# A list scheduler that prices changes of tile shape and GpSimd beside VectorE, and ranks the r, v and adaLN steps between units 3 and 4

## The chip, the cores and the metric

One core of a Trainium2 chip. The metric is the device time of one execution in microseconds; the kernel's time is the median of its runs.

## The reference

A decoder trunk of two layers on 256 tokens of width 1024, in float32. Each sub-layer's input is modulated by adaLN, and its output goes through a DeepNorm post-norm:

```
h = x * (1 + scale) + shift
x = LayerNorm(alpha * x + (1 + gate) * f(h))
```

Layer 0 has RWKV-7 time mixing and then a dense SwiGLU of width 2816. The time mixing, which the change is about, is

```
r, k, v = h @ w_rkv + shifted(h) @ w_lerp
w, a, g = three low-rank products of h
per head of 64:  state = state*decay + (state@-kk) kk*a + v k ;  y = state @ r
y = (normalize(y) + bonus) * g ;  out = y @ w_out
```

Then come a shared key and value projection, dilated attention in three groups of heads, and a mixture of 8 experts of width 3584, two for each token. The scale, shift and gate rows all come from one product of the condition vector with a large matrix (`ada_w`), row by row; they are called adaLN rows here, with an index.

## The kernel before, in words

Every product is made in float32 from three passes over halves: ScalarE casts a weight tile to `whi`, VectorE (in places GpSimd) subtracts to get `wlo`, and `mm3` multiplies hi by hi, lo by hi and hi by lo. Nearly every compute instruction is issued by one helper (line 190), loads by `load` (line 119), so the profile's lines don't tell the places apart; the tile names do.

The time mixing is cut into 8 units: four groups of four heads (`c_`), each with two token tiles of 128 (`t`). `unit` (line 869) is a generator; four lanes run at a time, so units 0 to 3 are a first wave, and 4 to 7 take lanes as they come free. A unit computes decay and gates (`sg`), the masked products of its chunk (`SM`), a triangular inverse by block steps (`E`, `T`, `X`), the state (`ST`), the output `Y`, its normalization (`ysum`, `yss`, then Newton steps in `yny` and `yna`), adds bonus and bias, multiplies with the gate product (in `psb`), transposes and leaves the halves `ygh` and `ygl`.

Beside the units run other generators. `rv_task` (line 1192) makes r and v from streamed weights (`x0` and `x2` operands). `ada_lane` (line 377) computes the adaLN rows 3, 4, 2 and 12 from `rawa` loads by `ada_pe` (line 321). `wo_task` (line 1229) is the product with w_out, 96 products in all, 12 for each of the eight row blocks `k`, into four banks of PSUM; block `k` needs `ygh` of units of group `k // 2`. It begins only when all v are there, the gate row is broadcast and the adaLN lane has finished (`ada_left`), whose bank it takes over. `splitter` and `loader` bring the weights of k, r, v and w_out in that order, two tiles ahead of the product. `pn_task` is the post-norm (`u`, `bnst`, `ln_*`, then `f_xh` and `f_xl`, the operands of the FFN), and the `f0` tasks make the first column block of the FFN. The rest of the FFN and the experts are in program order. Attention runs in a second list scheduling.

The order is set by `spin` (line 1324). Each generator yields the engine of its next step and the tiles that it needs. `spin` takes the step with the least estimated start; where starts are equal, as when an engine's queue is the limit, the least rank goes first. Ranks: units 0 to 7 by number, `rv_task` 100, `yg_task` 101, `wo_task` 102, `ada_lane` 103, and up to 110 for `f0`. Starts come from a model: `Engine.cost` (line 133) estimates each instruction's duration and a clock for each engine is kept. The model also keeps an estimate of TensorE's clock (`ham`), into which columns count, and `pick` uses the same starts where a step may go to one of several engines. What `spin` decides is fixed at build time as the order on each engine's queue.

```
best = ((at, order), k_)   # at: need[0].start(need[1:]), order: the rank
yield lambda: len(vsb) == 8 and "gate" in pre and not ada_left[0]   # wo_task
```

Of the kernel before, what the change touches and what calls it, by code (L numbers as in the profile page):

```python
# [91 lines left out]
def tile_kernel(ctx: ExitStack, tc: tile.TileContext, cst_d, att_d, x, c, ada_w, ada_b, ln_g, ln_b, mu, w_rkv,  # L92
# [4 lines left out]
    clk = {"PE": 0.0, "V": 0.0, "SC": 0.0, "GP": 0.0, "DMA": 0.0}  # L97
# [22 lines left out]

    TICK = 3413.0
    HAMT, LAT = 3250, 150
    ham = {"tick": 0, "n": 0, "warm": False, "col": -1}
    grp = {"all": 0.0}
    past = []

    class Engine:
# [5 lines left out]
        def cost(self, op, o, w, start):  # L133
            n = 1
            for d_ in o.shape[1:]:
                n *= d_
            if self.nm == "PE":
                passes = (2 if op == "transpose" else 4) if w.dtype == F32 else 1
                tick = start // TICK
                if tick != ham["tick"]:  # L140
                    ham["warm"] = tick == ham["tick"] + 1 and ham["n"] >= HAMT
                    ham["tick"], ham["n"] = tick, 0
                k, m, col = w.shape[0], o.shape[0], o.start_partition()
                cold = 1 if ham["warm"] else 2
                n0 = ham["n"]
                if m <= 64:
                    t0 = max(start, grp["all"], grp.get(col, 0.0))
                    alt = ham["col"] not in (-1, col)
                    ham["col"] = col
                    ham["n"] += passes * n * k / (128 if not alt else 256 if m > 32 else 512)  # L150
                    grp[col] = t0 + passes * max(n, m) / 2.4 * cold
                    past.append((t0, ham["n"] - n0))
                    return t0 - start + passes / 4 * (64 + n / 4) * cold
                ham["col"] = -1
                ham["n"] += passes * n * k / 128
                past.append((start, ham["n"] - n0))
                grp["all"] = max([start] + list(grp.values())) + passes * max(n, m) / 2.4 * 1.02 * cold
                return grp["all"] - start
            if op == "memset":
                return 60 + n * 0.8  # L160
            if self.nm == "V" and op == "reduce_sum":
                n = 256
            if self.nm == "SC":
                return 55 + n * 0.82 + (0 if op == "copy" else 80)
            return {"V": 70 + n / 0.96, "GP": 60 + n * 2.2 + (70 if n < 512 else 0)}[self.nm]

        def start(self, aps, o=None):
            return max([clk[self.nm]] + [rdy.get(r.tensor.name, 0.0) for r in aps] + (
# [1023 lines left out]
    def rv_task():  # L1192

        yield lambda: len(ksb) == 2
        for j, (kind, c_, i, q) in enumerate(parts):
# [6 lines left out]
                ps = mmt(RV.index((c_, i)) % 2, (128, 2, 256))  # L1202
                ps = [ps[:, 0], ps[:, 1]]
            yield lambda: xvn[i] > q * 4 + 3
            yield PE, hi, lo, xl, ps[0], ps[1]
            for k in range(4):
                kk = q * 4 + k
                for t in range(2):
# [115 lines left out]
    def spin(others, n_units=0, idle=None, ahead=()):  # L1324
# [5 lines left out]
        while True:  # L1330
# [7 lines left out]
            for k_, (order, g, need) in tasks.items():  # L1338
# [2 lines left out]
                    moved = True  # L1341
                if need is None or callable(need):
                    continue
                if isinstance(need[0], int):
                    order, need = need[0], need[1:]
                at = need[0].start(need[1:]) - (AHEAD if ahead and order in ahead else 0)
                if best is None or (at, order) < best[0]:
# [46 lines left out]
    with tc.manual_schedule(engines={mybir.EngineType.PE, mybir.EngineType.DVE, mybir.EngineType.Activation,  # L1394
                                     mybir.EngineType.Pool}):
        spin([(-5, mod_task()), (-4, kvar_task()), (-3, k_task()), (-2.2, splitter()), (51, loader()), (-4.5, lora_task()), (ORD[0], lorag_task()),
                 (ORD[1], rvvar_task(0)), (ORD[2], rvvar_task(2)), (100, rv_task()), (101, yg_task()), (102, wo_task()),
                 (103, ada_lane(LANE)), (104, pre_task()), (105, pn_task(0)), (106, pn_task(1)),
                 (107, f0_load_task()), (108, f0_split_task()), (109, f0_task(0)), (110, f0_task(1))], 8)
    bg_add(*[i for i in ADAS if i not in LANE + LATE])  # L1400
    a_stack.close()
# [24 lines left out]
    xh, xl = pre["fx"]  # L1426
# [808 lines left out]
```

## Time and profile before

| | |
|---|---|
| median of 3 runs | 1843.85 us (1843.07 to 1847.41) |
| profiled execution | 1846.92 us |
| its span | 1845.2 us |
| mean granted clock of TensorE | 0.964 |
| TensorE busy (weight loading) | 1715.7 us, 93% (1368.3 us, 74%) |
| VectorE, ScalarE, GpSimd busy | 1497.0, 1120.4 and 296.6 us |
| read from HBM | 496.07 MB |

The times in the rows are counted from the start of the span; the profiled execution is 3.07 us above the median and 1.7 us above its span. An idle time in front of an instruction stands in brackets, with what ended it. A granted clock of 1.00 is 2.4 GHz.

### The profile page before, as it was taken

How to read it: one execution, taken by the hardware profiler on the slowest of the kernel's cores; microseconds unless marked ns; L12 is line 12 of the kernel's file. 1: busy time of each engine (PE TensorE's matmuls, PEld its weight loads, DVE VectorE, ACT ScalarE, POOL GpSimd, SP SyncE). 2: the span in 40 equal slices, each digit the busy share in tenths (PEclk: the TensorE clock that was granted, in tenths of full speed). 3: DMA queues.
4: the chain of work that ended last, by engine and by line, in shares of the span. 5: the costliest groups of instructions: out<-in, count | busy, mean ns of one | idle time of the engine just before them, and what ended most of it. 6: DMA issues, size and time to landing. Idle time of an engine off the chain costs nothing. (4 is left out here: it accounts for less than half of the span.)

```text
span 1845.2 us, 26366 instructions
## 1 busy us (share of the span) xinstructions
PE 1715.7 (93%) x9828; PEld 1368.3 (74%) x9828; DVE 1497.0 (81%) x2044; ACT 1120.4 (61%) x1447; POOL 296.6 (16%) x222
## 2 busy tenths in 40 slices
PE   6998998869998888979999999999999999999896
PEld 3676776558876666778888888888788787788674
DVE  2786786389886768579899898998888988988888
ACT  3443342236553656438777777877777777777674
POOL 0012222044532785250000000000000000000200
PEclk8998998889998999979999999999999999999998
DMA  9551153559894574568999999999999999999880
GB/s 330 155 160 30 54 164 116 150 189 357 296 354 151 194 256 154 195 230 293 334 352 368 357 349 380 348 360 332 345 368 340 352 345 349 352 344 359 311 320 24
DMA packets 213564, 498.94 MB, mean 270 GB/s; under 512 B 14634, under 2 KB 28818, under 8 KB 213428
## 3 DMA queue, kind: packets, MB, share of 16 engines
q1 hardware_dynamic: 212564, 494.03, 75.7%
q0 software_dynamic: 864, 3.15, 0.5%
q8 instruction: 79, 1.29, 0.3%
q14 instruction: 57, 0.47, 0.1%
HBM read 496.07 MB, written 1.06 MB: 269 GB/s over the span
## 5 line engine op out<-in xcount | busy, mean ns | idle before, releaser
L190 DVE TENSOR_TENSOR wlo<-raw,whi 128x1024 fp32r<-128x1024 f32 x800 | 991.6, 1277 | 138.0 <-ACT whi L190 123.7
L190 ACT CAST whi<-raw 128x1024 fp32r<-128x1024 f32 x808 | 823.9, 1048 | 291.9 <-PE mmb L190 221.2
L190 PE MATMUL mmb<-wlo,xeh 128*128 128x512 f32 x896 | 355.9, 397 | 5.9 <-DVE wlo L190 5.2
L190 PE MATMUL mmb<-whi,xeh 128*128 128x512 f32 x896 | 352.5, 394 | 0.0
L190 PE MATMUL mmb<-whi,xel 128*128 128x512 f32 x896 | 351.6, 392 | 0.0
L190 PEld LDWEIGHTS mmb<-wlo,xeh 128*128 128x128 f32 x896 | 168.4, 188 | 48.3 <-DVE wlo L190 14.9
L190 PEld LDWEIGHTS mmb<-whi,xeh 128*128 128x128 f32 x896 | 168.4, 188 | 34.2 <-ACT whi L190 0.2
L190 PEld LDWEIGHTS mmb<-whi,xel 128*128 128x128 f32 x896 | 168.4, 188 | 32.6
L190 PE MATMUL psb<-wlo,ah 128*128 128x512 f32 x448 | 176.7, 394 | 1.5 <-DVE wlo L190 1.5
L190 PE MATMUL psb<-whi,al 128*128 128x512 f32 x448 | 174.7, 390 | 0.0
L190 PE MATMUL psb<-whi,ah 128*128 128x512 f32 x448 | 161.8, 391 | 0.0
L190 POOL TENSOR_TENSOR macc<-macc,gate 128x1024 f32<-128x1024 f32 x2 | 5.7, 2889 | 924.8 <-ACT gate L190 924.8
L190 POOL TENSOR_TENSOR acc<-acc,raw 128x512 f32<-128x512 f32 (+1 forms) x62 | 128.2, 2082 | 74.2 <-DVE acc L190 42.9
L190 PEld LDWEIGHTS psb<-wlo,ah 128*128 128x128 f32 x448 | 84.1, 188 | 24.6 <-DVE wlo L190 6.2
L190 PEld LDWEIGHTS psb<-whi,ah 128*128 128x128 f32 x448 | 83.5, 188 | 18.8 <-ACT whi L190 1.6
L190 PEld LDWEIGHTS psb<-whi,al 128*128 128x128 f32 x448 | 84.2, 188 | 16.4
L190 PE MATMUL mmb<-whi,f_xl 128*128 128x512 f32 (+1 forms) x192 | 72.1, 375 | 1.1 <-DVE f_xl L190 1.1
L190 PE MATMUL mmb<-whi,f_xh 128*128 128x512 f32 (+1 forms) x192 | 72.7, 379 | 0.0
L190 PE MATMUL mmb<-wlo,f_xh 128*128 128x512 f32 (+1 forms) x192 | 72.0, 375 | 0.2 <-DVE wlo L190 0.2
L190 ACT CAST ah<-psb 128x512 fp32r<-128x512 f32 x56 | 32.6, 583 | 60.3 <-PE psb L190 60.2
L190 ACT ACTIVATE e_s<-mmb 128x512 f32<-128x512 f32 x56 | 33.5, 599 | 44.8 <-PE mmb L190 44.8
L190 DVE TENSOR_TENSOR e_s<-e_s,mmb 128x512 f32<-128x512 f32 x56 | 38.2, 683 | 22.5 <-PE mmb L190 22.2
(417 smaller groups left out, 2589.3 us busy)
## 6 DMA issues: line engine op xcount, KB each, us to landing
raw<-in_moe_w_gu_dram SPq DMA_DIRECT2D x192, 1024.0 KB, 6.6
raw<-in_moe_w_down_dram SPq DMA_DIRECT2D x83, 1024.0 KB, 6.1
raw<-in_moe_w_gu_dram SPq DMA_DIRECT2D x60, 512.0 KB, 7.0
raw<-in_moe_w_down_dram SPq DMA_DIRECT2D x56, 512.0 KB, 6.0
raw<-in_ada_w_dram SPq DMA_DIRECT2D x37, 512.0 KB, 5.3
rawa<-in_ada_w_dram SPq DMA_DIRECT2D x35, 512.0 KB, 4.2
raw<-in_ada_w_dram SPq DMA_DIRECT2D x15, 1024.0 KB, 7.8
raw<-in_ffn_w_gu_dram SPq DMA_DIRECT2D x21, 512.0 KB, 5.3
```

Source lines behind the costliest of these rows:

```text
L190: return fn(*a, **kw)
```

## The change

Two things change; what is computed stays the same. First, the scheduler's model. On TensorE 170 ns are added whenever the class of the tile's shape (rows and columns of the weights: up to 32, up to 64, or 128) differs from that of the product before. Products into alternating column groups count in full towards the estimate of the clock, where they counted for a half or a quarter. An operation on VectorE is estimated longer by 0.6 of the time for which GpSimd's estimated work reaches into it. Second, the ranks: the product steps of `rv_task` and all steps of `ada_lane` go from 100 and 103 to 3.5, and `spin` takes a rank that is no integer. Both list schedulings are drawn up anew by this model, attention's too.

```
--- before.py
+++ after.py
@@ -120,6 +120,7 @@
 
     TICK = 3413.0
     HAMT, LAT = 3250, 150
+    CHG, GPF = 170, 0.6
     ham = {"tick": 0, "n": 0, "warm": False, "col": -1}
     grp = {"all": 0.0}
     past = []
@@ -143,26 +144,38 @@
                 k, m, col = w.shape[0], o.shape[0], o.start_partition()
                 cold = 1 if ham["warm"] else 2
                 n0 = ham["n"]
-                if m <= 64:
-                    t0 = max(start, grp["all"], grp.get(col, 0.0))
-                    alt = ham["col"] not in (-1, col)
-                    ham["col"] = col
-                    ham["n"] += passes * n * k / (128 if not alt else 256 if m > 32 else 512)
-                    grp[col] = t0 + passes * max(n, m) / 2.4 * cold
-                    past.append((t0, ham["n"] - n0))
-                    return t0 - start + passes / 4 * (64 + n / 4) * cold
-                ham["col"] = -1
-                ham["n"] += passes * n * k / 128
-                past.append((start, ham["n"] - n0))
-                grp["all"] = max([start] + list(grp.values())) + passes * max(n, m) / 2.4 * 1.02 * cold
-                return grp["all"] - start
+                shp = tuple(32 if v <= 32 else 64 if v <= 64 else 128 for v in (k, m))
+                if shp != ham.get("shape"):
+                    ham["shape"] = shp
+                    start0, start = start, start + CHG
+                    grp["all"] = max([grp["all"]] + list(grp.values())) + CHG
+                    return self.pe(op, o, passes, n, k, m, col, cold, n0, start) + CHG
+                return self.pe(op, o, passes, n, k, m, col, cold, n0, start)
             if op == "memset":
                 return 60 + n * 0.8
             if self.nm == "V" and op == "reduce_sum":
                 n = 256
             if self.nm == "SC":
                 return 55 + n * 0.82 + (0 if op == "copy" else 80)
-            return {"V": 70 + n / 0.96, "GP": 60 + n * 2.2 + (70 if n < 512 else 0)}[self.nm]
+            if self.nm == "V":
+                d_ = 70 + n / 0.96
+                return d_ + GPF * min(d_, max(0.0, clk["GP"] - start))
+            return 60 + n * 2.2 + (70 if n < 512 else 0)
+
+        def pe(self, op, o, passes, n, k, m, col, cold, n0, start):
+            if m <= 64:
+                t0 = max(start, grp["all"], grp.get(col, 0.0))
+                alt = ham["col"] not in (-1, col)
+                ham["col"] = col
+                ham["n"] += passes * n * k / 128
+                grp[col] = t0 + passes * max(n, m) / 2.4 * cold
+                past.append((t0, ham["n"] - n0))
+                return t0 - start + passes / 4 * (64 + n / 4) * cold
+            ham["col"] = -1
+            ham["n"] += passes * n * k / 128
+            past.append((start, ham["n"] - n0))
+            grp["all"] = max([start] + list(grp.values())) + passes * max(n, m) / 2.4 * 1.02 * cold
+            return grp["all"] - start
 
         def start(self, aps, o=None):
             return max([clk[self.nm]] + [rdy.get(r.tensor.name, 0.0) for r in aps] + (
@@ -1202,7 +1215,7 @@
                 ps = mmt(RV.index((c_, i)) % 2, (128, 2, 256))
                 ps = [ps[:, 0], ps[:, 1]]
             yield lambda: xvn[i] > q * 4 + 3
-            yield PE, hi, lo, xl, ps[0], ps[1]
+            yield 3.5, PE, hi, lo, xl, ps[0], ps[1]
             for k in range(4):
                 kk = q * 4 + k
                 for t in range(2):
@@ -1341,7 +1354,7 @@
                     moved = True
                 if need is None or callable(need):
                     continue
-                if isinstance(need[0], int):
+                if isinstance(need[0], (int, float)):
                     order, need = need[0], need[1:]
                 at = need[0].start(need[1:]) - (AHEAD if ahead and order in ahead else 0)
                 if best is None or (at, order) < best[0]:
@@ -1395,7 +1408,7 @@
                                      mybir.EngineType.Pool}):
         spin([(-5, mod_task()), (-4, kvar_task()), (-3, k_task()), (-2.2, splitter()), (51, loader()), (-4.5, lora_task()), (ORD[0], lorag_task()),
                  (ORD[1], rvvar_task(0)), (ORD[2], rvvar_task(2)), (100, rv_task()), (101, yg_task()), (102, wo_task()),
-                 (103, ada_lane(LANE)), (104, pre_task()), (105, pn_task(0)), (106, pn_task(1)),
+                 (3.5, ada_lane(LANE)), (104, pre_task()), (105, pn_task(0)), (106, pn_task(1)),
                  (107, f0_load_task()), (108, f0_split_task()), (109, f0_task(0)), (110, f0_task(1))], 8)
     bg_add(*[i for i in ADAS if i not in LANE + LATE])
     a_stack.close()
```

The compiled orders show what it moves. TensorE around unit 4's first products, which are those into `psb` from `w2t` with `lw` and `a2t` with `la` (the first number behind `SV`, `SM`, `U`, `T`, `E` or `Y` is the unit's, a last one of three or four digits tells buffers apart; `x2h` and `x2l` are operands of the v projection). Before:

```order
L190 MATMUL psb_1902<-ART_3_1399,BKT_3_1839 128x128 x4
L190 MATMUL psb_1927<-SV_2_1913,SM_2_1421 64x64 x4
L190 MATMUL psb_1938<-w2t_265,lw_267 128x256
L190 MATMUL psb_1938<-a2t_266,la_268 128x256
L190 MATMUL psb_1951<-U_2_1918,E_2_1529 64x64 x4
L190 MATMUL psb_1961<-T_3_1949,SM_3_1854 64x64 x8
L190 MATMUL psb_1972<-g2t_868,lga_269 128x256
L190 MATMUL psb_1972<-w2t_265,lw_267 128x256
L190 MATMUL psb_1977<-SV_2_1913,BKn_2_1233 128x128 x2
L190 MATMUL psb_1981<-cst_79,Y_1_1715 128x128 x2
```

and with the change:

```order
L203 MATMUL mmb_2222<-whi_2187,x2h_256 128x256
L203 MATMUL mmb_2222<-wlo_2188,x2h_256 128x256
L203 MATMUL mmb_2222<-whi_2187,x2l_257 128x256
L203 MATMUL psb_2348<-w2t_265,lw_267 128x256
L203 MATMUL psb_2348<-a2t_266,la_268 128x256
L203 MATMUL psb_2356<-w2t_265,lw_267 128x256
L203 MATMUL psb_2356<-a2t_266,la_268 128x256
L203 MATMUL mmb_617<-cst_79,row_2365 128x128 x2
L203 MATMUL psb_2373<-U_3_2255,E_3_1646 64x64 x4
```

Before, unit 4 begins among the steps of units 2 and 3, and 144 of the 384 products of r and v come behind it. With the change all of them are ahead: unit 4 begins behind the last v product, with unit 5 beside it, and next to it stands one of unit 3's late steps.

TensorE around unit 7's end: the last adaLN products (`rawa`), the first ones of w_out (`ygh`, `ygl`) and the transposes of unit 7's output (`cst` with `Y_7`). Before:

```order
L190 MATMUL mmb_3698<-rawa_3837,cs_act_96 32x256 x4
L190 MATMUL mmb_3698<-rawa_3860,cs_act_96 32x256 x4
L190 MATMUL mmb_3698<-cst_79,row_3892 128x128 x2
L190 MATMUL mmb_3901<-whi_2666,ygh_1125 128x512
L190 MATMUL mmb_3901<-wlo_2667,ygh_1125 128x512
L190 MATMUL mmb_3901<-whi_2666,ygl_1126 128x512
L190 MATMUL psb_3910<-g2t_868,lga_269 128x256
L190 MATMUL psb_3910<-w2t_265,lw_267 128x256
L190 MATMUL mmb_3902<-whi_2666,ygh_1125 128x512
L190 MATMUL mmb_3902<-wlo_2667,ygh_1125 128x512
L190 MATMUL mmb_3902<-whi_2666,ygl_1126 128x512
L190 MATMUL psb_3917<-cst_79,Y_7_3763 128x128 x2
```

and with the change:

```order
L203 MATMUL mmb_3531<-whi_3986,ygh_1264 128x512
L203 MATMUL mmb_3531<-wlo_3987,ygh_1264 128x512
L203 MATMUL mmb_3531<-whi_3986,ygl_1265 128x512
L203 MATMUL mmb_3532<-whi_3966,ygh_1264 128x512
L203 MATMUL mmb_3532<-wlo_3967,ygh_1264 128x512
L203 MATMUL mmb_3532<-whi_3966,ygl_1265 128x512
L203 MATMUL mmb_3532<-whi_3986,ygh_1264 128x512
L203 MATMUL mmb_3532<-wlo_3987,ygh_1264 128x512
L203 MATMUL mmb_3532<-whi_3986,ygl_1265 128x512
L203 MATMUL psb_4037<-g2t_835,lga_269 128x256
L203 MATMUL psb_4037<-w2t_265,lw_267 128x256
L203 MATMUL psb_4046<-cst_79,Y_7_3817 128x128 x2
```

Before, the adaLN products are followed by w_out's first two sets of three and then by unit 7's transposes, and 90 of the 96 products of w_out come behind. With the change no adaLN product is left here, and these w_out products are the last of the first token tile; 12 products, all of the second tile, come behind the transposes.

VectorE around unit 7's end: `wlo` are the splits of w_out's tiles (the last two of the FFN's), `u0` is the post-norm. Before:

```order
L190 TENSOR_TENSOR Y_7_3763<-Y_7_3763,psb_3910 128x256
L190 TENSOR_TENSOR ygl_1126<-psb_3917,ygh_1125 128x2x128
L190 TENSOR_TENSOR wlo_3929<-raw_2709,whi_3928 128x1024
L190 TENSOR_TENSOR wlo_3947<-raw_2784,whi_3946 128x1024
L190 TENSOR_TENSOR wlo_3971<-raw_3938,whi_3970 128x1024
L190 TENSOR_TENSOR wlo_3986<-raw_3956,whi_3985 128x1024
L190 TENSOR_TENSOR wlo_4007<-raw_3977,whi_4006 128x1024
L190 TENSOR_TENSOR wlo_4020<-raw_3995,whi_4019 128x1024
L190 TENSOR_TENSOR u0_4043<-mmb_3901,gate1_3699 128x512
L190 SCALAR_TENSOR_TENSOR u0_4043<-xres_3260,u0_4043 128x512
L190 TENSOR_TENSOR wlo_4038<-raw_4023,whi_4037 128x1024
```

and with the change, from unit 6's last steps on, and then the end of unit 7:

```order
L203 TENSOR_TENSOR wlo_3902<-raw_3857,whi_3901 128x1024
L203 TENSOR_TENSOR ygl_1265<-psb_3922,ygh_1264 128x2x128
L203 TENSOR_REDUCE ysum_7_3961<-Y_7_3817 128x4
L203 TENSOR_SCALAR ysum_7_3961<-ysum_7_3961 128x4
L203 TENSOR_TENSOR Y_7_3817<-Y_7_3817,ysum_7_3961 128x256
L203 TENSOR_TENSOR wlo_3967<-raw_3890,whi_3966 128x1024
...
L203 TENSOR_TENSOR Y_7_3817<-Y_7_3817,vsb1_2675 128x256
L203 TENSOR_TENSOR u0_4035<-mmb_3531,gate1_3455 128x512
L203 TENSOR_TENSOR Y_7_3817<-Y_7_3817,psb_4037 128x256
L203 SCALAR_TENSOR_TENSOR u0_4035<-xres_3405,u0_4035 128x512
L203 TENSOR_TENSOR wlo_4042<-raw_4005,whi_4041 128x1024
L203 TENSOR_TENSOR ygl_1265<-psb_4046,ygh_1264 128x2x128
```

Before, six splits stand between `ygl` of unit 7 and the first step on `u0`. With the change splits stand between the steps of units 6 and 7, and the first step on `u0` stands ahead of the last steps of unit 7. On the load queue (SP) w_out's last four tiles stay behind all adaLN loads and behind that of `bb`, as they were behind the adaLN loads before.

## Rows read from the trace of the kernel before

**Rows 1.** Stretches of the span: columns are stretch and its length, then as named

```profile
core 0: us, PE busy (x) PEld busy (x) DVE busy (x) ACT busy (x) POOL busy (x), PEclk, DMA share, GB/s
59.00:180.00 121.00, 109.67 (x1153) 88.37 (x1152) 89.28 (x244) 47.63 (x113) 18.58 (x32) 0.95 0.39 117
180.00:294.00 114.00, 103.69 (x1287) 81.67 (x1286) 89.48 (x289) 43.59 (x113) 28.50 (x45) 0.94 0.34 107
294.00:345.00 51.00, 43.32 (x471) 29.29 (x472) 18.91 (x67) 12.26 (x33) 7.25 (x13) 0.78 0.46 136
...
394.00:584.00 190.00, 187.74 (x926) 153.78 (x924) 153.76 (x134) 102.26 (x120) 69.09 (x28) 1.00 0.82 299
...
823.00:1832.00 1009.00, 997.85 (x4575) 813.01 (x4574) 898.62 (x858) 754.39 (x821) 12.42 (x4) 1.00 0.92 332
```

**Rows 2.** Timeline of ScalarE, first instruction of units 0 and 4 (start, duration, instruction)

```profile
59.46 0.38 ACT L190 ACTIVATE sg<-psb 128x256 f32<-128x256 f32 x1 [0.52 <-PE psb L190]
...
180.41 0.39 ACT L190 ACTIVATE sg<-psb 128x256 f32<-128x256 f32 x1 [1.18 <-PE psb L190]
```

**Rows 3.** Timeline of VectorE, first inverse step of unit 7

```profile
293.52 0.76 DVE L190 STREAM_TRANSPOSE T<-E 128x256 f32<-128x256 f32 x2
```

**Rows 4.** Timeline of VectorE, 345 to 394 us

```profile
345.18 0.42 DVE L190 TENSOR_TENSOR ygl<-psb,ygh 128x256 fp32r<-128x256 f32 x1 [1.99 <-ACT ygh L190]
348.12 1.23 DVE L190 TENSOR_TENSOR wlo<-raw,whi 128x1024 fp32r<-128x1024 f32 x1 [2.52 <-ACT whi L190]
...
362.66 1.22 DVE L190 TENSOR_TENSOR wlo<-raw,whi 128x1024 fp32r<-128x1024 f32 x1 [1.39 <-ACT whi L190]
364.71 0.69 DVE L190 TENSOR_TENSOR u<-mmb,gate 128x512 f32<-128x512 f32 x1 [0.82 <-PE mmb L190]
...
366.14 1.22 DVE L190 TENSOR_TENSOR wlo<-raw,whi 128x1024 fp32r<-128x1024 f32 x1
...
369.21 1.22 DVE L190 TENSOR_TENSOR wlo<-raw,whi 128x1024 fp32r<-128x1024 f32 x1
...
370.95 0.67 DVE L190 TENSOR_TENSOR u<-mmb,gate 128x512 f32<-128x512 f32 x1
...
393.14 0.84 DVE L190 TENSOR_TENSOR f_xl<-modtmp,f_xh 128x512 fp32r<-128x512 f32 x1 [0.69 <-ACT f_xh L190]
```

**Rows 5.** Timeline of TensorE, 337 to 379 us

```profile
337.19 1.08 PE L190 MATMUL mmb<-rawa,cs_act 128*32 128x256 f32 x8 [2.01 <-DMA rawa<-in_ada_w_dram]
...
339.10 0.78 PE L190 MATMUL mmb<-whi,ygh 128*128 128x512 f32 x1
...
368.21 0.39 PE L190 MATMUL mmb<-wlo,ygh 128*128 128x512 f32 x1
368.45 0.40 PE L190 MATMUL mmb<-whi,ygl 128*128 128x512 f32 x1
378.27 1.11 PE L190 MATMUL psb<-cst,u 128*128 128x128 f32 x4 [9.43 <-DVE u L190]
```

**Rows 6.** Groups of TensorE's instructions, 294 to 372 us (busy us, mean ns, idle before)

```profile
L190 PE MATMUL mmb<-whi,ygh 128*128 128x512 f32 x32 | 14.1, 440 | 0.6 <-ACT whi L190 0.6
L190 PE MATMUL mmb<-wlo,ygh 128*128 128x512 f32 x32 | 13.7, 427 | 1.0 <-DVE wlo L190 1.0
L190 PE MATMUL mmb<-whi,ygl 128*128 128x512 f32 x32 | 13.3, 415 | 0.0
L190 PE MATMUL mmb<-rawa,cs_act 128*32 128x256 f32 x104 | 10.1, 465 | 4.8 <-DMA rawa<-in_ada_w_dram 4.8
```

**Rows 7.** Timeline of VectorE, with GpSimd busy beside it and without

```profile
277.97 0.83 DVE L190 SCALAR_TENSOR_TENSOR sg<-kQ,sg 128x256 f32<-128x256 f32 x1
278.83 0.42 DVE L190 TENSOR_TENSOR kQ<-kQ 128x256 f32<-128x256 f32 x1
```

**Rows 8.** Waits of TensorE's weight loading, 60 to 370 us (total, times, longest)

```profile
PEld psb L190 <- issue: 29.4, 70, 2.0
```

**Rows 9.** Timelines of VectorE and GpSimd near the end of attention

```profile
792.54 8.48 DVE L190 SCALAR_TENSOR_TENSOR ln_a<-ln_y,ln_v 128x1 f32<-128x1 f32 x1
...
791.15 4.69 POOL L190 TENSOR_TENSOR wlo<-raw,whi 128x1024 fp32r<-128x1024 f32 x2
```

## The prediction

> **What bounds the kernel now.** I read the table of stretches first [rows 1]. From 394 to 584 us (the FFN) TensorE is busy 187.74 of 190 us, and from 823 to 1832 us (the experts) 997.85 of 1009, both at a granted clock of 1.00, 2.4 GHz. Both are written in program order and are not rearranged, so whatever moves their first product moves the end by the same amount. The time to win or lose lies in the two list-scheduled parts, up to 394 us and 764 to 823 us.
>
> In the first part I read the milestones of the units. Unit 0 begins at 59.46 us and unit 4, which opens the second wave, at 180.41 (their sigmoids on ScalarE) [rows 2]. Unit 7 starts its triangular inverse at 293.52 [rows 3]. Then I followed VectorE from there [rows 4]: unit 7's result is split into its halves at 345.18. Only after that come six splits of w_out, the first at 348.12, the last at 362.66, and at 364.71 the first `u` of the post-norm. The last operand of the FFN (`f_xl`) ends at 393.14 + 0.84 = 393.98. So from unit 7's result to the first `u` is 364.71 - 345.18 = 19.5 us, in which VectorE does 6 x 1.23 us and otherwise waits, 2.52 us before the first.
>
> Why is w_out so late? TensorE's list [rows 5] has the last adaLN products at 337.19, behind a wait of 2.01 us for their load, and the first product with `ygh` at 339.10. `wo_task` starts only when the adaLN lane is finished. That gate, not the data, set the start: on four lanes, unit 7 can only begin when units before it are done, so w_out's first rows had long been there. TensorE then idles 9.43 us before 378.27, waiting for `u`.
>
> **The change, part by part.**
> *Planner numbers.* They compute nothing and cost nothing on the chip; they only alter the order. Five operations go from ScalarE to VectorE, and attention gets 24 more of the dummy products that keep the clock up, all in TensorE's waits: 0.
>
> *Ranks.* The r, v and adaLN steps now go ahead of units 4 to 7 when TensorE could take either. Counting the compiled orders (a 4-byte product is two records), 1249 records lay between the first products of unit 0 and unit 4, now 1538; between there and unit 7's inverse 1234, now 1041; from there to its final transposes 455, now 437; from there to the first FFN product 118, now 32. The adaLN products are all before unit 7's inverse, so w_out is let go there: of its 96 products 90 came behind unit 7's transposes, now 12.
>
> Term 1, the gap. From `ygl` of unit 7 to `u` 19.5 us goes, and the two later splits (366.14 and 369.21, 1.22 us each, between steps of the layer norm) [rows 4] go too: -19.5 - 2.4 = **-21.9 us**. As a check the other way round: what must follow `ygl` now is 12 products and token tile 1's half of the post-norm. The 12 cost at most 12 x 0.44 = 5.3 us by the longest mean [rows 6], say 4; from tile 1's first `u` at 370.95 to 393.98 is 23.0 us [rows 4]. Together 27 of the 48.8 us that it takes now: -21.4.
>
> Term 2, the splits put elsewhere. Six of the eight splits now stand between steps of units 6 and 7 on VectorE. Each is 1.23 us [rows 4] and, where it waits for its cast or load, holds what is queued behind it: the unit's Newton steps. Bounds 0 (in VectorE's waits: it is busy 18.91 of 51 us from 294 to 345 [rows 1]) and 6 x 1.23 = 7.4; half of them on the path: **+3.7 us**.
>
> Term 3, more work ahead of unit 7. Net 96 records come in front of its inverse, in the main the 104 adaLN products: 10.1 us by their row [rows 6] if nothing hides them. TensorE idles 121 - 109.67 = 11.3 us in the first wave and 114 - 103.69 = 10.3 in the second [rows 1], so some of it fills gaps: bounds 0 and 10.1, I take **+4 us**.
>
> Term 4, w_out's products between unit 7's steps. Each set of three delays a small product by at most its own time, 27 sets in all; against it, the adaLN waits such as 2.01 us are gone and the clock of 0.78 in that stretch [rows 1] should rise with more work. I set these against each other: 0. Here rows can be read in two ways. By TensorE's busy time, 43.32 of 51 us [rows 1], only 7.7 us are free for products that take at least (14.1 + 13.7 + 13.3) / 96 x 81 = 34.7 us of busy time at the mean of [rows 6], or 81 x 0.23 = 18.6 us by their spacing at the full clock (the last two begin at 368.21 and 368.45 [rows 5]). By weight loading, 29.29 of 51, there are 21.7 us free. The first reading would give back 18.6 - 7.7 = 10.9 us, the second none; I take the second, since the unit's small products overlap one another. The Trainium skill (Trainium Kernel Development and Optimization, section Performance Expectations) says that matmul busy time is a bad metric because matmuls are pipelined and that the busy share of weight loading is a good one; by that rule the term stays 0, and no row here alone settles it.
>
> Tile shapes: by the new rule's classes the order of the first part has 227 changes instead of 240. What a change costs no row shows alone; the nearest is TensorE's weight loading waiting for nothing but issue, 29.4 us in 70 waits, 0.42 each [rows 8]. 13 x 0.42 = 5.5 us at most, 0 at least; I take 0, since these waits lie on a unit's own chain too. The Trainium skill (TensorEngine Tiling (Array Packing), section Key Properties) says a change of tiling mode drains the engine, which would put the value nearer to the 5.5.
>
> VectorE beside GpSimd: the same kind of 256-wide operation takes 0.83 us beside GpSimd and 0.42 without [rows 7]. The new price steers splits and adds, but not the units' own GpSimd steps, and the VectorE instructions up to unit 7's inverse are 592 in both orders: 0, at best some 5 us.
>
> Term 5, attention. The adds of the last adaLN rows move, the out-projection of the second token tile stands behind the router of the first, and three normalizations move to GpSimd. The end of attention already has such a stall: a tiny VectorE operation took 8.48 us at 792.54 while GpSimd was splitting weights from 791.15 [rows 9]. Such a stall can go (-8.3) or come again; the order of neither shows which. **0**, bounds -5 and +8.
>
> Sum: -21.9 + 3.7 + 4 + 0 + 0 = **-14.2 us**. The profiled execution took 1846.92 us (span 1845.2 and 1.7 around it), so it would be 1832.7; it stands 3.07 above the median, so against that **1830 us**.
>
> **The rivals.**
> A, slower: the second wave starts late and does not catch up. 289 more records before unit 4, at 109.67 / 1153 = 0.095 us each [rows 1], are 27.5 us, or 30 at that stretch's busy share of 0.91. If the second wave then still takes its 113 us, because the chain of each unit and not TensorE's queue sets it, and has no r, v or adaLN products to fill its waits, unit 7's inverse is at 324 instead of 293.5. Then +30 - 18 = +12: 1856 us. For it: VectorE was busy 89.48 of those 114 us [rows 1], and its unit work is the same; with units 4 and 5 starting together near unit 3's end, fewer units are under way at the seam to fill one another's waits. Against it: TensorE is busy 103.69 of 114, so its queue counts, and 193 records fewer are worth 193 x 0.081 = 15.6 us. It decides once the inverse begins after 294 + 18 = 312 us. Chance 0.14.
>
> B, little gained: w_out is let go but takes TensorE's time from unit 7 (10.9 us given back, above), or its loads come late: its last four stand behind 19 adaLN loads on SP's queue and behind one of `bb`, which waits for a buffer that unit 7 still reads. -14.2 + 10.9 = -3.3, or half of it; between 1834 and 1841. Chance 0.22.
>
> C, more: the steps of the second wave also run better, with 5.5 us of tile changes and some 7 us of VectorE's doubled operations gone: 1830 - 12.5 = 1817. Chance 0.14.
>
> D, the change of order eats its own gain in attention: +8 there, 1838. Chance 0.08. That it does not do what it says is excluded by the order, which moves as its words tell.
>
> **How the numbers follow.** The forecast has 0.42, rivals A to D 0.14, 0.22, 0.14 and 0.08. What counts as no change is 0.3%, 5.5 us: the fence is 1838.3. The forecast falls below it in nearly all cases (0.40), C in all (0.14), B in seven of ten (0.15), D in half (0.04), together 0.73; A is above 1849.4, nearly all of it slower: 0.13; the rest, 0.14, lies between. The range, 1813 to 1848, holds the forecast with its bounds (-27 and -2), B, D and C, and leaves out A and a better C.
>
> **What would show it.** Unit 4's first sigmoid near 205 us; unit 7's inverse near 298; w_out's splits and products inside unit 6 and 7's steps, with hardly a wait between unit 7's `ygl` and `u`; the first full stretch of the FFN 14 us earlier; the experts unchanged in length. An inverse after 312, a split that waits several us for its load ahead of unit 7's Newton steps, or an attention stage 8 us longer would make it wrong.

## The result, and the profile after

The changed kernel takes 1856.3 us (median of 4 runs, 1854.97 to 1859.77), 1.0054 times the kernel before (95% interval 1.0034 to 1.0074). The forecast was 1830 us and the range 1813 to 1848: wrong in sign and outside the range, and at the time that rival A gave, 1856 us. The execution profiled here took 1859.77 us, with a span of 1858.0 us, 12.8 above that of before.

The table of stretches of the changed kernel, with the columns of [rows 1], cut at its own milestones:

```profile
core 0: us, PE busy (x) PEld busy (x) DVE busy (x) ACT busy (x) POOL busy (x), PEclk, DMA share, GB/s
60.00:180.00 120.00, 109.74 (x1140) 90.04 (x1139) 87.61 (x228) 45.37 (x108) 20.75 (x32) 0.93 0.35 105
180.00:215.00 35.00, 34.31 (x403) 29.92 (x402) 20.12 (x58) 14.86 (x33) 4.62 (x8) 1.00 0.49 163
215.00:325.00 110.00, 89.82 (x1009) 62.14 (x1008) 71.25 (x246) 31.73 (x90) 23.45 (x38) 0.84 0.44 135
325.00:361.00 36.00, 34.87 (x402) 26.63 (x403) 19.88 (x52) 13.86 (x32) 6.29 (x10) 1.00 0.19 60
...
404.00:594.00 190.00, 188.02 (x928) 154.37 (x927) 153.02 (x133) 101.27 (x120) 67.99 (x27) 1.00 0.82 299
...
835.00:1845.00 1010.00, 998.35 (x4574) 813.14 (x4574) 897.98 (x856) 753.48 (x819) 12.40 (x4) 1.00 0.92 332
```

The FFN (404 to 594 us) and the experts (835 to 1845) are as full and as long as they were in [rows 1]; they begin later. From 180 to 215 us TensorE is full, 34.31 of 35 us. Then come 110 us in which it has less work than before (1009 products, where 180 to 294 us had 1287), at a granted clock of 0.84, and VectorE is busy 71.25 us of them. Here the wave that began late does not catch up.

ScalarE's timeline has the first sigmoids of units 0, 4 and 7 ([rows 2] has those of 0 and 4 before):

```profile
60.24 0.38 ACT L203 ACTIVATE sg<-psb 128x256 f32<-128x256 f32 x1 [0.21 <-PE psb L203]
...
214.92 0.38 ACT L203 ACTIVATE sg<-psb 128x256 f32<-128x256 f32 x1
...
293.78 0.38 ACT L203 ACTIVATE sg<-psb 128x256 f32<-128x256 f32 x1 [0.44 <-PE psb L203]
```

Unit 4 begins 34.5 us later than before, and unit 7 only at 293.78. VectorE's timeline has the first inverse step of unit 7, and then the end of the first part, to hold against [rows 3, 4]:

```profile
324.57 0.45 DVE L203 STREAM_TRANSPOSE T<-E 128x256 f32<-128x256 f32 x1
...
363.05 1.23 DVE L203 TENSOR_TENSOR wlo<-raw,whi 128x1024 fp32r<-128x1024 f32 x1 [1.20 <-ACT whi L203]
...
365.83 1.23 DVE L203 TENSOR_TENSOR wlo<-raw,whi 128x1024 fp32r<-128x1024 f32 x1 [0.21 <-ACT whi L203]
...
371.25 0.68 DVE L203 TENSOR_TENSOR u<-mmb,gate 128x512 f32<-128x512 f32 x1
...
373.92 0.42 DVE L203 TENSOR_TENSOR ygl<-psb,ygh 128x256 fp32r<-128x256 f32 x1
...
383.56 0.68 DVE L203 TENSOR_TENSOR u<-mmb,gate 128x512 f32<-128x512 f32 x1
...
403.02 0.93 DVE L203 TENSOR_TENSOR f_xl<-modtmp,f_xh 128x512 fp32r<-128x512 f32 x1 [0.69 <-ACT f_xh L203]
```

The inverse is 30.7 us late (of the two transposes in [rows 3] the second is unit 7's, at 293.88). From there to the end of the last `f_xl` it is now 403.95 - 324.57 = 79.4 us, where it was 100.1. The splits of w_out lie ahead of unit 7's `ygl` (373.92), and the first `u` stands even before it. So the tail gave about what was forecast; the part before it took more than that.

The waits from 215 to 325 us (engine and tile, what it waited for, total, times, longest), and five of the adaLN products in TensorE's timeline:

```profile
DVE E L203 <- PE psb L203: 22.8, 6, 9.5
...
PEld mmb L203 <- DMA rawa<-in_ada_w_dram: 13.0, 11, 2.7
...
PE mmb L203 <- DMA rawa<-in_ada_w_dram: 11.0, 9, 2.4
```

```profile
256.28 0.64 PE L203 MATMUL mmb<-rawa,cs_act 128*32 128x256 f32 x8 [0.73 <-DMA rawa<-in_ada_w_dram]
...
259.56 1.08 PE L203 MATMUL mmb<-rawa,cs_act 128*32 128x256 f32 x8 [2.03 <-DMA rawa<-in_ada_w_dram]
...
268.27 0.64 PE L203 MATMUL mmb<-rawa,cs_act 128*32 128x256 f32 x8 [0.63 <-DMA rawa<-in_ada_w_dram]
...
271.54 0.64 PE L203 MATMUL mmb<-rawa,cs_act 128*32 128x256 f32 x8 [2.26 <-DMA rawa<-in_ada_w_dram]
...
283.62 1.08 PE L203 MATMUL mmb<-rawa,cs_act 128*32 128x256 f32 x8 [2.42 <-DMA rawa<-in_ada_w_dram]
```

TensorE, which works through its queue in order, stands before adaLN products whose loads have not landed: 11.0 us by the products, 13.0 by the weight loads, of the same waits. Before, such waits for products came to 4.8 us, all of them behind 294 us [rows 6]. In the same 110 us VectorE waits 22.8 us for what the inverse needs (`E`). The longest of these waits, 9.5 us up to 286.63 us, spans the adaLN products at 279.98 and 283.62, for whose loads TensorE waited 0.90 and 2.42 us; e9 below shows how much of the 22.8 us is left without such waits. The load queue shows the pace of the loads:

```profile
238.03 47.06 SPq L119 DMA_DIRECT2D rawa<-in_ada_w_dram  x17
```

In 47 us it issues 17 loads of 512 KB, one in 2.9 us from the first to the last: there are two `rawa` buffers (`RAWA` is 2), and a load can start only when the product on its buffer is done. No run has another number of buffers.

Last, the first product of the experts, in the kernel before and now:

```profile
822.84 0.48 PE L190 MATMUL mmb<-whi,xeh 128*128 128x512 f32 x1
```

```profile
835.24 0.47 PE L203 MATMUL mmb<-whi,xeh 128*128 128x512 f32 x1 [1.27 <-DVE xel L203]
```

From the end of `f_xl` to there it was 428.9 us and is 431.3: FFN and attention give away 2.4, FFN at equal length. In sum, 12.4 of the 12.8 us of span:

| | before | after | difference |
|---|---|---|---|
| unit 4 begins | 180.4 | 214.9 | +34.5 |
| from there to unit 7's inverse | 113.5 | 109.7 | -3.8 |
| from there to the last `f_xl` | 100.1 | 79.4 | -20.7 |
| from there to the experts | 428.9 | 431.3 | +2.4 |

### The profile page after: what moved, and what is told of

The parts are those of the page before. It is cut to its first block, busy times and chain, and to the rows that moved or that the text cites. A ratio compares the mean times of both kernels' runs of the same rounds, so it can differ in the third digit from the quotient of the medians.

```text
span 1858.0 us, 26409 instructions
## 1 busy us (share of the span) xinstructions
PE 1724.7 (93%) x9852; PEld 1374.3 (74%) x9852; DVE 1499.7 (81%) x2049; ACT 1117.3 (60%) x1442; POOL 295.9 (16%) x222
## 5 line engine op out<-in xcount | busy, mean ns | idle before, releaser
L203 DVE TENSOR_TENSOR e_s<-e_s,mmb 128x512 f32<-128x512 f32 x56 | 38.3, 684 | 22.3 <-PE mmb L203 21.9
```

Of the source, the lines that this page charges most:

```text
L203: return fn(*a, **kw)
```

## The experiments

Two theories first. S: r and v, ranked ahead of units 4 to 7, make the second wave late, and its chains set the rest. L: the adaLN products, ranked ahead too, bind TensorE's queue to the pace of their loads. A third, M, blames the new prices. As redrawn orders differ everywhere, the last runs ask what a nudge alone does. The table has every run; 3.5 is the rank of the change, late is 100 or 103, and the times after the ratio are of its profile: unit 4's start, unit 7's inverse, the end of the last `f_xl`, the first expert product. The kernel before had medians from 1844.3 to 1848.2 us beside the different runs, so of two times in us that are compared below some 4 us mean nothing.

| run | prices | r, v | adaLN | ratio to before (95%) | unit 4 | inverse | `f_xl` | experts |
|---|---|---|---|---|---|---|---|---|
| before | old | late | late | 1 | 180 | 294 | 394 | 823 |
| the change | new | 3.5 | 3.5 | 1.0054 (1.0034 to 1.0074) | 215 | 325 | 404 | 835 |
| e1 | new | 3.5 | late | 1.0093 (1.0060 to 1.0126) | 204 | 307 | 408 | 837 |
| e2 | new | late | 3.5 | 0.9905 (0.9869 to 0.9942) | 171 | 299 | 378 | 806 |
| e3 | new | late | late | 1.0207 (1.0169 to 1.0244) | 183 | 319 | 430 | 861 |
| e4 | old | 3.5 | 3.5 | 1.0085 (1.0057 to 1.0112) | 201 | 327 | 410 | 835 |
| e5 | old | late | 3.5 | 0.9999 (0.9986 to 1.0012) | 187 | 321 | 395 | 824 |
| e6 | old | 3.5 | late | 1.0051 (1.0034 to 1.0068) | 200 | 310 | 399 | 828 |
| e7 | new | 3.6 | 3.5 | 1.0100 (1.0082 to 1.0117) | 187 | 329 | 412 | 841 |
| e8 | new | 5.5 | 3.5 | 0.9933 (0.9912 to 0.9954) | 174 | 311 | 390 | 813 |
| e9 | as the change, loads cut | 3.5 | 3.5 | 0.9962 (0.9941 to 0.9982) | 214 | 307 | 386 | 817 |
| e10 | new, no tile price | late | 3.5 | 0.9839 (0.9809 to 0.9868) | 178 | 297 | 373 | 791 |
| e11 | new, no GpSimd price | late | 3.5 | 1.0032 (1.0013 to 1.0052) | 178 | 311 | 396 | 830 |
| e12 | new | 3.5, last group 5.5 | 3.5 | 1.0007 (0.9992 to 1.0022) | 207 | 314 | 393 | 820 |
| e13 | new, no tile price | 3.5 | 3.5 | 0.9938 (0.9922 to 0.9953) | 183 | 314 | 394 | 813 |
| e14 | the change, 150 ns | 3.5 | 3.5 | 1.0113 (1.0092 to 1.0134) | 213 | 330 | 411 | 846 |
| e15 | e2, 150 ns | late | 3.5 | 0.9947 (0.9928 to 0.9967) | 171 | 309 | 391 | 812 |
| e16 | e10, factor 0.5 | late | 3.5 | 0.9876 (0.9855 to 0.9896) | 179 | 298 | 375 | 799 |
| e17 | no tile price in attention | 3.5 | 3.5 | 1.0023 (1.0002 to 1.0044) | 215 | 322 | 401 | 825 |
| e18 | new, no tile price | 5.5 | 3.5 | 0.9862 (0.9836 to 0.9888) | 180 | 286 | 373 | 798 |

**One part of the change at a time (e1 to e4).** Edits of the changed kernel; e3 has both, and e4 is the kernel before with both ranks set to 3.5.

```
e1  -(3.5, ada_lane(LANE))           +(103, ada_lane(LANE))
e2  -yield 3.5, PE, hi, lo, xl, ...  +yield PE, hi, lo, xl, ...
```

> The changed kernel with the adaLN lane back at rank 103; r and v stay at 3.5, the model stays new. Theory L (the adaLN products at 3.5 hold TensorE's queue at the pace of their loads in the second wave, 24 us of waits for the loads between 215 and 300 us): those waits are gone, unit 4 still begins near 215, unit 7's inverse comes at about 300 instead of 324.6, w_out starts late again, so the FFN's operands end about 100 us after the inverse, at 400: 1852 us or a little less. Theory S (r and v ahead of unit 4 make the wave start 34 us late, and the chain of the units sets the rest): the inverse stays at 320 or later and, with w_out late again, 1870 us or more.

> The changed kernel with the r and v products back at rank 100; the adaLN lane stays at 3.5, the model stays new. Theory S: unit 4 begins near 180 again, the inverse of unit 7 comes near 295 and the early w_out keeps its 18 to 20 us: 1830 us. Theory L: adaLN products still hold the queue, now earlier and beside more work; the inverse comes at 310 or later, 1845 us or more.

> Both ranks back at 100 and 103; only the new prices (170 ns for a change of tile shape, GpSimd beside VectorE, columns counted in full) stay. Theories L and S: the ranks are the cause, so 1840 to 1848 us, with unit 7's inverse near 294 and the w_out products behind it. Theory M (the new prices fill TensorE's queue in the model, steps tie, and the higher units are pushed back whatever the ranks are): inverse at 310 or later, 1855 us or more.

> The kernel before with only the two ranks set to 3.5; the old prices. Theories L and S: as the change, 1852 to 1860 us, unit 4 near 210, the inverse of unit 7 at 315 to 325, w_out ahead of unit 7's transposes. Theory M: the units are not pushed back, inverse near 300, 1830 to 1840 us.

e2 took 1830.66 us, as S said, below the change and below the kernel before: with r and v back at the end alone, the early adaLN keeps the short tail and the second wave begins in time. Its rows, unit 4's sigmoid and unit 7's inverse, then the first product of w_out, then the first `u` and the last `f_xl`:

```profile
170.55 0.38 ACT L203 ACTIVATE sg<-psb 128x256 f32<-128x256 f32 x1 [0.19 <-PE psb L203]
...
299.13 0.45 DVE L203 STREAM_TRANSPOSE T<-E 128x256 f32<-128x256 f32 x1
```

```profile
301.57 0.50 PE L203 MATMUL mmb<-whi,ygh 128*128 128x512 f32 x1
```

```profile
347.42 0.68 DVE L203 TENSOR_TENSOR u<-mmb,gate 128x512 f32<-128x512 f32 x1
...
377.46 0.84 DVE L203 TENSOR_TENSOR f_xl<-modtmp,f_xh 128x512 fp32r<-128x512 f32 x1 [0.69 <-ACT f_xh L203]
```

e1 took 1862.5 us, between the two times expected, and its inverse came at 307, between L's 300 and S's 320: without the adaLN products in front the second wave needs 103 us in place of 110, and the tail is long again (101 us). That is what one would see if both have a share; e9 below splits them. e4 (1861.58 us, 1.6 above the range of L and S) shows that both ranks together cost as much under the old prices.

e3 took 1885.44 us, with the inverse at 319: what M expected, and neither S nor L. (In e4 M fails.) Its rows show the last copy of v and the first product of w_out:

```profile
305.30 0.66 ACT L203 COPY vsb<-mmb 128x256 f32<-128x256 f32 x2
...
376.22 0.78 PE L203 MATMUL mmb<-whi,ygh 128*128 128x512 f32 x1
```

v is finished at 306 us (before at 247) and w_out begins at 376. With the new prices it is not the higher units but the steps of the last ranks, r and v and the adaLN lane, that come late. So the new prices need new ranks; alone they cost 2%. Why these two starve no run takes apart.

**Tie or place (e5 to e8).** e5 and e6 complete the pairs under the old prices; e7 and e8 change the 3.5 of r and v in the change.

```
e7  -yield 3.5, PE, hi, lo, xl, ...  +yield 3.6, PE, hi, lo, xl, ...
e8  -yield 3.5, PE, hi, lo, xl, ...  +yield 5.5, PE, hi, lo, xl, ...
```

> The kernel before with the adaLN lane at 3.5 alone: r and v at 100, old prices. Theory S (only r and v ahead of unit 4 do harm; the early adaLN frees w_out): unit 4 near 180, unit 7's inverse near 300, w_out ahead of unit 7's end, 1828 to 1838 us, as the run with new prices and r and v late (1830.7). Theory M' (the adaLN rank helps only together with the new prices): 1845 us or more.

> The kernel before with r and v at 3.5 alone: adaLN at 103, old prices. Theory S: unit 4 near 205, the inverse of unit 7 at 315 or later, w_out late as before, 1865 us or more. If r and v did harm only through a tie with the adaLN steps at the same rank: unit 4 near 185 and 1840 to 1850 us.

> The changed kernel with r and v at 3.6 in place of 3.5: still ahead of units 4 to 7, but behind the adaLN lane, with which they tied. Theory S: still late, the second wave behind r and v, 1850 to 1862 us. Theory T (what did harm is that r and v, listed first, win their ties against the adaLN steps): 1828 to 1835 us, as with r and v at 100.

> The changed kernel with r and v at 5.5: behind units 4 and 5, ahead of 6 and 7. Theory S: units 4 and 5 begin near 175, so 1826 to 1836 us; what is left of the harm falls on units 6 and 7. Theory T: 1830 us as well. If any rank ahead of a unit costs its full delay: 1840 us or more.

T falls: e7, without the tie, took 1864.41 us, 2 above S's range; its unit 4 begins at 187, but unit 5 at 220. S holds in e8 (1831.38 us): behind units 4 and 5, r and v do no harm that shows in the time, though the inverse is 12 us later than in e2. Under the old prices r and v early cost less: 0.5% with adaLN late (e6, 1853.84 us, in neither range expected) and 0.9% with adaLN early (e5 against e4). e5 (1846.61 us) is a miss for S and what M' expected: the tail is short, 75 us, but the inverse comes at 321, and the two cancel. Why it comes so late there is open: unit 7 begins at 252 as before, and TensorE's products wait only 5.6 us for adaLN loads.

**The loads, and what each price does (e9 to e12).** e9 keeps the change's order on every engine and cuts each load of the adaLN lane to a quarter; the rest of the row is left out, and the model goes on counting the full load.

```
e9   -load(rw, ada_w[rows, idx * D:(idx + 1) * D])
     +SY.dma_start(rw[:, 0:256], ada_w[rows, idx * D:idx * D + 256])
     -rws[q][:, g * 256 + c0:g * 256 + c0 + n]  +rws[q][:, c0:c0 + n]
e10  e2 and  -CHG, GPF = 170, 0.6  +CHG, GPF = 0, 0.6
e11  e2 and  -CHG, GPF = 170, 0.6  +CHG, GPF = 170, 0.0
e12  -yield 3.5, PE, ...  +yield 3.5 if c_ < 3 else 5.5, PE, ...
```

> The changed kernel with the same order on every engine, but each load of the adaLN lane brings only 256 of its 1024 columns and all four products of a row block read these (the other three quarters are left out, so the scale, shift and gate rows of the first layer hold repeated values). Theory L (the second wave does not catch up because TensorE's queue stands at the adaLN loads): the waits for these loads (11 us of product and 13 of weight loading) shrink below 4 us, unit 7's inverse comes 10 us or more earlier, at 315 or before, 1846 us or less. Theory S (the late start of units 4 and 5 and their own chains set it): the waits go, but the inverse stays at 319 or later, 1851 to 1858 us.

> The best run so far (new prices, adaLN at 3.5, r and v at 100, 1830.7 us) without the 170 ns for a change of tile shape. If that price makes the gain over the same ranks with old prices (1846.6): 1840 to 1850 us, and more changes of shape on TensorE. If the GpSimd price or the column count makes it: 1828 to 1835 us.

> The best run so far without the price for GpSimd beside VectorE (factor 0 in place of 0.6). If that price makes the gain: 1840 to 1850 us. If the price for tile shapes makes it: 1828 to 1835 us.

> The changed kernel with r and v of the last head group, which only units 6 and 7 read, at 5.5; those of the others stay at 3.5. Theory S: unit 4 begins near 190 in place of 215 and half of the harm goes, 1838 to 1850 us. If what counts is any r or v product ahead of units 4 and 5: as the change, 1852 us or more.

e9 took 1842.26 us, 14 below the change. The adaLN products from 215 to 300 us in its trace and in that of the change (count | busy us, mean ns | idle before), then unit 4's and unit 7's rows of e9, and what VectorE waits for `E` there from 215 to 325 us:

```profile
L203 PE MATMUL mmb<-rawa,cs_act 128*32 128x256 f32 x192 | 16.4, 415 | 0.0
```

```profile
L203 PE MATMUL mmb<-rawa,cs_act 128*32 128x256 f32 x192 | 18.9, 473 | 11.0 <-DMA rawa<-in_ada_w_dram 11.0
```

```profile
213.88 0.38 ACT L203 ACTIVATE sg<-psb 128x256 f32<-128x256 f32 x1
...
306.94 0.45 DVE L203 STREAM_TRANSPOSE T<-E 128x256 f32<-128x256 f32 x1
```

```profile
DVE E L203 <- PE psb L203: 11.7, 8, 4.8
```

The same 192 products wait for no load now, unit 4 begins as late as in the change, and the inverse is 17.6 us earlier. So S and L are both true, and this run, whose order is that of the change, splits them: the wave begins 34 us late, would make up 113.5 - 93.1 = 20.4 us of it (unit 4's start to unit 7's inverse, before and in e9), and gives 16.6 back at the loads. That is more than the 11.0 us of waits in front of the products; VectorE's waits for `E` fall from 22.8 to 11.7, and the granted clock from 215 to 300 us is 0.90 where it was 0.84. What the clock has of the 16.6 is not taken apart. The price of the loads also hangs on the order: in e2 the lane has the same rank, but r and v are in the wave with it; there TensorE's products wait 7.4 us for loads in the whole first part, and the last adaLN product is at 234 us, 65 us ahead of the inverse (in the change at 290, 35 ahead).

e10 took 1817.16 us, the fastest of all and below both times expected: the price for tile shapes makes no gain, it costs time (e2 has it, 1830.66). The price for GpSimd does make one: without it 1854.63 us (e11), more than the 1840 to 1850 expected. How the columns are counted has no run of its own. e12, 1847.28 us, has a third of the 25.6 us between the change and e2 gone, with unit 4 at 207, later than expected.

**Place or draw (e13 to e18).**

```
e13  -CHG, GPF = 170, 0.6  +CHG, GPF = 0, 0.6
e14  -CHG, GPF = 170, 0.6  +CHG, GPF = 150, 0.6      e15  the same in e2
e16  e10 and  -CHG, GPF = 0, 0.6  +CHG, GPF = 0, 0.5
e17  170 in a list, CHGS, and ahead of the second spin:  +CHGS[0] = 0
e18  e10 and  -yield PE, ...  +yield 5.5, PE, ...
```

> The changed kernel without the 170 ns for a change of tile shape; r, v and adaLN stay at 3.5. Theory S (r and v ahead of units 4 and 5 do the harm, whatever the prices): 1835 to 1850 us, 20 us or more above the same prices with r and v at 100 (1817.2), with units 5 to 7 beginning 15 us or more later than there. Theory P (the price for tile shapes does it): 1815 to 1825 us.

> The changed kernel with 150 in place of 170 ns, a nudge that should mean nothing by itself. Theories S and L: the order shifts a little, 1850 to 1862 us. Theory Z (each new order is a draw, with a spread as large as the differences seen between the runs): anything from 1825 to 1885 us, outside 1846 to 1866 as likely as in it.

> The run with new prices, adaLN at 3.5 and r and v at 100 (1830.7 us), with 150 in place of 170 ns. Theory S: 1822 to 1838 us, below every run with r and v at 3.5. Theory Z: anything from 1815 to 1870 us.

> The fastest run (no price for tile shapes, adaLN at 3.5, r and v at 100, 1817.2 us) with a factor of 0.5 in place of 0.6 for GpSimd. Theory S, with the GpSimd price doing its part: 1812 to 1826 us. Theory Z: anything from 1810 to 1860 us.

> The changed kernel with the 170 ns for a change of tile shape dropped in the second list scheduling (attention) alone; the order up to the FFN is that of the change. If the price's harm in attention is what the runs without it show (10 to 12 us between the FFN's operands and the first expert product: 431.3 us in the change, 418.9 and 418.4 without the price): the first part as in the change, operands at 404, and 1842 to 1848 us. If those 10 us came from what the first part hands over: 1853 to 1859 us.

> The fastest run (no price for tile shapes, adaLN at 3.5, r and v at 100, 1817.2 us) with r and v at 5.5, behind units 4 and 5 and ahead of 6 and 7. Theory S: as with the tile price, where 5.5 and 100 came out alike (1831.4 and 1830.7): 1812 to 1826 us, units 4 and 5 begin as in that run, near 178 and 193. If every unit that r and v are put ahead of costs: 1827 us or more.

A nudge that should mean nothing moves the time by 11.8, 5.9 and 5.9 us (e14 to e16: 1868.06, 1836.52, 1823.11 us), upwards each time. e14 is outside the range of S and L and inside Z's (which had values outside 1846 to 1866 as likely as those in it); e15 and e16 are in the ranges of both. So there is a draw in each order, as large as what the change as a whole did (12.0 us); the far ends that Z allowed were not reached. Against it stand r and v early less late: 25.6 us (the change and e2), 31.5 (e14 and e15), 18.4 (e13, 1835.57 us, and e10). These three are beyond the spread, and so are the GpSimd price's 24 us, though they are one pair only. Under the old prices the same difference, 15.0 us (e4 and e5) and 8.2 (e6 and before), is at the spread's edge or in it. e13 is in S's range, but its 18.4 us fall short of the 20 expected, and of units 5 to 7 only 5 and 6 begin late (214 and 234 us, in e10 193 and 206); unit 7 begins at 245 in place of 243. Nor is e15 below every run with r and v early, as S had it: e13, at another price, is 1 us faster. Only with adaLN late and new prices does it go the other way (e1 is 22.9 us faster than e3), since r and v come so late there by themselves. The tile price's 13.5 and 20.7 us are near its edge and above it, and of one sign.

Part of the tile price's cost may lie in attention. Unit 4, unit 7's inverse, last `f_xl` and first expert product of e10, and the last two of e17:

```profile
178.27 0.38 ACT L203 ACTIVATE sg<-psb 128x256 f32<-128x256 f32 x1 [0.26 <-PE psb L203]
...
296.72 0.45 DVE L203 STREAM_TRANSPOSE T<-E 128x256 f32<-128x256 f32 x1
...
367.21 5.57 DVE L203 TENSOR_TENSOR f_xl<-modtmp,f_xh 128x512 fp32r<-128x512 f32 x2 [0.69 <-ACT f_xh L203]
```

```profile
791.21 0.47 PE L203 MATMUL mmb<-whi,xeh 128*128 128x512 f32 x1
```

```profile
400.01 0.92 DVE L204 TENSOR_TENSOR f_xl<-modtmp,f_xh 128x512 fp32r<-128x512 f32 x1 [0.69 <-ACT f_xh L204]
```

```profile
824.57 0.48 PE L204 MATMUL mmb<-whi,xeh 128*128 128x512 f32 x1
```

From the end of `f_xl` (372.78 and 400.93 us) it is 418.4 us in e10 and 423.6 in e17, against 431.3 in the change. Over all the runs with the new model it is 418.4 to 425.2 us without the price in attention and 421.4 to 435.0 with it; the old model, which had no such price, has 425.4 to 428.9. e17 took 1850.24 us, in neither of the two ranges expected: dropping the price in attention brings 6 of the 20.7 us, which is no more than a nudge does. Nor is all of that attention's: with the order of the change up to the FFN, e17's `f_xl` ends 3.0 us earlier. Where the rest lies is open, since e13's first part is 10 us shorter as well, by another order. e18 took 1822.15 us, as S said.

## Why the prediction was wrong

- **Term 1, the gap behind unit 7 (-21.9) and term 2 (+3.7):** right in mechanism, and near in sum: forecast -18.2, measured -20.7. Taken apart, they miss to both sides. From unit 7's `ygl` to the end of the last `f_xl` it was 48.8 us and is 403.95 - 373.92 = 30.0, not the 27 of the check, so 18.8 us were won and not 21.9; from its inverse to `ygl`, where the splits now stand, 1.9 us were won and not 3.7 lost. From unit 7's inverse to the last `f_xl` every run with adaLN early has 75 to 87 us, and those with it late 89 to 111.
- **Term 3, more work ahead of unit 7 (+4, at most 10.1):** this is the step that failed. The inverse came 30.7 us late. I priced it as work, net 96 records, with TensorE's idle time to take it up, and so let the wave make up its late start in full. Two things are not work. Units 4 and 5 have no start until the r and v products are through, +34.5 us, near rival A's 30. And the order ties the wave to the loads, +16.6 us by e9. My split of the records was wrong as well: the 1249 and 1538 run to the first product that reads a unit's `sg`, not to its first product. To that one the orders have 1185 and 1573, so 388 more in place of 289, and between it and unit 7's inverse 292 fewer in place of 193; the net stays 96. At rival A's 0.095 and 0.081 us these are 36.9 and 23.7 us, near the 34.5 by which unit 4 begins late and the 20.4 that the wave makes up in e9.
- **Term 4:** "the adaLN waits such as 2.01 us are gone" was false. They moved with their products into the second wave and grew from 4.8 to 11 us: 192 records now stand there, at the pace of loads into two buffers, where 104 stood behind 294 us. [rows 5] had already shown the wait; I did not ask what sets the pace of these loads. The clock did rise where w_out was put in, to 1.00 from 325 to 361 us, but it is 0.84 in the 110 us of waits before, where it was 0.94 [rows 1]. The other half of the term held: from unit 7's inverse to its `ygl` it was 51.3 us (345.18 - 293.88) and is 49.4 (373.92 - 324.57), with 81 products of w_out in between, where there were 6. So nothing was given back, as the second reading had it. But this does not decide between the readings, since the 104 adaLN records (10.1 us [rows 6]) left the same stretch and its clock went from 0.78 to 1.00; TensorE is busy 34.87 of the 36 us from 325 to 361 and weight loading 26.63. That fits what the Trainium skill (Trainium Kernel Development and Optimization, section Performance Expectations) says of the two, but no run here tests it.
- **Tile shapes and GpSimd:** both set to 0. As prices in the plan they are not: the GpSimd one is worth 24 us (e11 against e2, one pair), and that for tile shapes costs 13 to 21. None of it is the hardware's price of a change of shape, which no run isolates. The Trainium skill (TensorEngine Tiling (Array Packing), section Key Properties) says that a change of tiling mode drains the engine, which no run here shows; a plan that counts it was slower all the same.
- **Term 5, attention (0, -5 to +8):** FFN and attention together +2.4, within the bounds.
- **The rivals:** A was right in place and point of decision (an inverse after 312 us), and its late start was real. That its price was met is luck: it let the wave take its full 113 us because the units' chains set it, with no adaLN products in it. But 192 adaLN records are in it, and without their waits the wave makes up 20.4 us (e9). The r and v early and the early adaLN were one decision to me. Taken apart, under the new prices, r and v early are a loss of about 26 us (e2). The adaLN lane early is a gain of 54.8 us with r and v late (e2 against e3), but of 6.2 with r and v early (the change against e1), which is within the spread; under the old prices it gains nothing (e5).

## What to carry to other kernels

Price a step that is ranked ahead not only as work but by who may not start until it is through and by what it waits for: in a queue that works in order, a product whose load is paced by two buffers passes its wait on to everything behind it. When several ranks move together, look at each by itself; here one undid what the other won, and the version that moves only the adaLN rank and leaves out the price for tile shapes, with the rest of the new model (e10), takes 0.984 of the time before. And before reading a cause into a redrawn order, nudge a number that should not matter: 6 to 12 us came from nothing else.

## What the runs showed of the hardware

Loads of 512 KB into two buffers, each waiting for the product on the buffer, came at one in 2.9 us (17 in 47.06 us) in the second wave, each landing 3.8 us after its issue (median). The same products with a quarter of the bytes, which landed in 2.1 us, did not wait at all. Nothing else was unexpected of the chip itself; the surprises were the order's.
